# Where the quadrant sums of a split-precision trunk are computed: 128 additions of 128x512 elements between GpSimd and VectorE

## The chip, the core and the metric

One core of one Trainium2 chip runs the whole program. The metric is device time in microseconds (us) of one execution, as the median of several. An engine name in a row is one of PE (TensorE's matmuls), PEld (TensorE's weight loads), DVE (VectorE), ACT (ScalarE), POOL (GpSimd) and SP (SyncE, which here issues the DMAs).

## What is computed

One layer of a trunk on 1024 tokens of 1024 channels, all in fp32:

```python
h = rms_norm(x, norm_mix_pre)
y = hybrid_mixer(h, w_in, ...)          # four mixers on one input projection, gates, w_out
x = x + rms_norm(y, norm_mix_post)
h = rms_norm(x, norm_ffn_pre)
gt, up = split(h @ w_ffn_in, 2)
x = x + rms_norm((silu(gt) * up) @ w_ffn_out, norm_ffn_post)
```

The input projection has 6912 columns (`w_in`), the FFN 2816 hidden channels. Each `rms_norm` multiplies by a factor per channel at its end.

## The kernel before

**Precision.** Every fp32 operand of a matmul is split in two (`split`, L133 to L137): ACT casts it to a reduced type (`hi`, L135), DVE subtracts that from the source (`lo`, L136), and three matmuls (hi by hi, hi by lo, lo by hi; L210 to L212, in the last product L1226 to L1228) take the place of one. So each operand costs an ACT cast and then a DVE subtraction before PE can use it. The split of a weight goes into a ring of three buffers (`whi`, `wlo`), so it can be at most three units of weights ahead of PE.

**Strassen's form.** Most of the two large products (from `w_in` and `w_ffn_in`) and all of the last one (`w_ffn_out`) are computed in Winograd's form of Strassen's method: seven block products in place of eight, on sums and differences of quadrants. Those sums are elementwise work. Three places make them.

- `token_sums` (L277 to L304) makes the four sums T1 to T4 of the tokens' quadrants, in four steps. A step adds the hi and lo of four quadrants back together into `x11`, `x12`, `x22`, `x21` (L296, four instructions), combines them on DVE (L297 to L300), and splits the four results (L136, tiles `T1h`, `T1l` and so on). It runs twice: at the start of the input projection (about 22 to 78 us in the profile) and at the start of the FFN (868 to 950 us). It runs interleaved with plain projections, whose weights (`wlo_av` of `raw_av`, and `wlo_fu` of `raw_fu`) are split by the same two engines.
- `column_sums` (L307 to L320) makes the sums of the weights for `wino`; that stays on POOL (L318).
- `ffn_out` (L1165 on) computes the last product. It takes the 22 blocks of 128 hidden channels as 11 pairs, in three chunks of 4, 4 and 3 pairs. In a chunk, `pairs_` holds two tiles `af` of activations and two of weights (`wf`, or `raw_fo` for the first two) for each pair, and a pair's operands are 128x512 quadrants A11 to A22 and B11 to B22. Seven products m1 to m7 follow each other; each takes one unit per pair (`units`: the split of one A and one B quadrant into `whi_fo`, `wlo_fo`) and 12 matmuls per unit. After the first product `sums1` (L1192) makes four sums of the pair (L1196 to L1199), and after the second `sums2` (L1202) four more (L1205 to L1208); the other five products use those. A finished product is added to `ya`, the result, by DVE (L1260) or in the first chunk partly copied by ACT (L1258).

In the last chunk the end of the layer is interleaved: when a half (512 channels) of a token tile is complete, `half_done` (L1266) takes its sum of squares on ACT (L1270), multiplies it by the channel factors `gf` of the last norm (L1271: the first half of a tile on POOL, the second on DVE), computes the reciprocal root on POOL (L1274, L1280, L1282), scales and adds the residual on DVE (L1285), and SP stores it (L1286).

**Order.** A scheduler sorts the instructions of each engine when the program is built; each engine then goes through its own queue strictly in that order. Priorities steer it: `tc.high_priority(n)` lets code be placed as if it had been written n steps earlier (AHEAD_SPLIT = 160 for splits and for the sums of `ffn_out`, AHEAD_SUM = 400 for `column_sums`). So when an operation changes its engine, the order around it changes too.

Of the kernel before, what the change touches and what calls it, by code (L numbers as in the profile page):

```python
# [13 lines left out]
ALU = mybir.AluOpType  # L14
# [24 lines left out]
def hybrid_trunk(ctx, tc, x, w_in, w_branch, w_out, w_ffn_in, w_ffn_out, cols, gpost, gfpost,  # L39
                 abias, wst, bsr, wabd, wxbd, lvl, tril, eye, out, dbg=None):  # L40
    nc = tc.nc
# [38 lines left out]
    def slot(name, dt=F32, w=D):  # L80
        cnt[0] += 1
        t = sp.tile([P, D], dt, tag="S", name=f"{name}_{cnt[0]}", bufs=NSLOT)
        return t[:, :w]
# [17 lines left out]
    def small(name, w):  # L101
        cnt[0] += 1
        return sm.tile([P, w], F32, tag=f"s{w}", name=f"{name}_{cnt[0]}", bufs={1: 24, 8: 8}.get(w, 4))
# [29 lines left out]
    def split(src, hi, lo, scale=None):  # L133
        if scale is None:
            nc.scalar.copy(hi, src)  # L135
            return nc.vector.tensor_tensor(lo, src, hi.bitcast(F32), op=ALU.subtract)  # L136
        else:  # L137
            nc.scalar.activation(hi, src, AF.Copy, scale=scale)
            return nc.vector.scalar_tensor_tensor(lo, src, scale, hi.bitcast(F32), op0=ALU.mult, op1=ALU.subtract)
# [129 lines left out]
    halfs = [slice(0, 512), slice(512, 1024)]  # L269

    def wtmp(name, dt=F32):
        cnt[0] += 1
        return scope["p"].tile([P, 512], dt, tag="w", name=f"{name}_{cnt[0]}", bufs=8)

    def b_quad(zs, i, j):
        return [lambda kk, z=z: z(4 * (i - 1) + kk, halfs[j - 1]) for z in zs]

    def token_sums(ops, *zs):
        T = {}
        for n in ("B11", "B12", "B21", "B22"):  # L280
            ops[n] = b_quad(zs, int(n[1]), int(n[2]))
        for n in ("T1", "T2", "T3", "T4"):
            T[n] = {}
            ops[n] = [lambda kk, n=n, z=z: T[n][kk // 2][z][:, (kk % 2) * 512 : (kk % 2) * 512 + 512] for z in range(2)]
        for kk in range(4):
            if kk % 2 == 0:
                for n in T:
                    T[n][kk // 2] = (slot(f"{n}h", F32R), slot(f"{n}l", F32R))

            def q(name, z):  # L290
                return ops[name][z](kk).bitcast(F32)


            x11, x12, x22, x21 = (wtmp(f"x{n}") for n in ("11", "12", "22", "21"))
            for n, t in (("B11", x11), ("B12", x12), ("B22", x22), ("B21", x21)):
                nc.gpsimd.tensor_tensor(t, q(n, 0), q(n, 1), op=ALU.add)  # L296
            nc.vector.tensor_tensor(x12, x12, x11, op=ALU.subtract)  # L297
            nc.vector.tensor_tensor(x22, x22, x12, op=ALU.subtract)
            nc.vector.tensor_tensor(x11, x22, x11, op=ALU.subtract)
            nc.vector.tensor_tensor(x21, x22, x21, op=ALU.subtract)  # L300
            t1, t2, t3, t4 = x12, x22, x11, x21
            for n, t in zip(T, (t1, t2, t3, t4)):
                last[1] = split(t, ops[n][0](kk), ops[n][1](kk))
            yield  # L304
# [625 lines left out]
    interleave(first_norm(), proj_tm("bi", copy_to))  # L930
    started.append(1)
    interleave(seq(proj_tm("av", copy_to), proj_tm("cv", twice_gelu)), token_sums(ops1, hTh, hTl), 2, 1)

    away = {}
# [233 lines left out]
    def ffn_out(chunk, first, final):  # L1168
        n = len(chunk)
        pairs_ = []  # L1170
        for i, p in enumerate(chunk):
# [12 lines left out]
            q = {}  # L1184
            for nm, t in (("A", a), ("B", w)):
                for u in range(2):
                    for h in range(2):
                        r, c_ = (h, u) if nm == "A" else (u, h)
# [2 lines left out]

        def sums1(q):  # L1192
            q["S1"], q["T2"] = wtmp("s1"), wtmp("t2")
            gt_ = nc.gpsimd.tensor_tensor
            with tc.high_priority(AHEAD_SPLIT):
                gt_(q["S1"], q["A21"], q["A22"], op=ALU.add)  # L1196
                gt_(q["A11"], q["S1"], q["A11"], op=ALU.subtract)  # L1197
                gt_(q["B11"], q["B12"], q["B11"], op=ALU.subtract)
                gt_(q["T2"], q["B22"], q["B11"], op=ALU.subtract)  # L1199
            q["S2"], q["T1"] = q["A11"], q["B11"]  # L1200

        def sums2(q):  # L1202
            gt_ = nc.gpsimd.tensor_tensor
            with tc.high_priority(AHEAD_SPLIT):
                gt_(q["A21"], q["A22"], q["S2"], op=ALU.subtract)  # L1205
                gt_(q["B12"], q["B22"], q["B12"], op=ALU.subtract)
                gt_(q["A12"], q["A12"], q["S2"], op=ALU.subtract)  # L1207
                gt_(q["B21"], q["B21"], q["T2"], op=ALU.subtract)  # L1208
            q["S3"], q["T3"], q["S4"], q["T4n"] = q["A21"], q["B12"], q["A12"], q["B21"]
# [56 lines left out]
        def half_done(tt, c_, second):  # L1266

            y = yacc[tt][:, halfs[c_]]
            ss = small("yss", 1)
            nc.scalar.activation(junk[:, :512], y, AF.Square, accum_out=ss)  # L1270
            (nc.vector if second else nc.gpsimd).tensor_tensor(y, y, gf[:, halfs[c_]], op=ALU.mult)  # L1271
            if not second:
                early[tt] = small("ms0", 1)
                nc.gpsimd.tensor_scalar(early[tt], ss, 1.0 / D, EPS, op0=ALU.mult, op1=ALU.add)  # L1274
                xts_[tt] = slot("x1b")
                with tc.high_priority(AHEAD_OUT):
                    nc.sync.dma_start(xts_[tt], x1s[tt])
                return
            ms = small("ms", 1)
            nc.gpsimd.tensor_scalar(ms, ss, 1.0 / D, early[tt], op0=ALU.mult, op1=ALU.add)  # L1280
            r = small("rstd", 1)
            nc.gpsimd.tensor_tensor(r, ms, neghalf[:, :1], op=ALU.pow)  # L1282
            for cs in (halfs[1 - c_], halfs[c_]):
                xt = xts_[tt][:, cs]
                nc.vector.scalar_tensor_tensor(xt, yacc[tt][:, cs], r, xt, op0=ALU.mult, op1=ALU.add)  # L1285
                nc.sync.dma_start(out[tt * P : (tt + 1) * P, cs], xt)  # L1286
# [4 lines left out]
        def into_last(r, c_, second):  # L1291

            ev = into(r, c_, (r, c_) == (0, 1))

            def evl(t, ps):
                ev(t, ps)
                if final:
                    half_done(4 * r + t, c_, second)

            return evl  # L1300
# [4 lines left out]
        m4 = lambda: prod(ps2, "A22", "T4n", into_last(1, 0, True), more=True)  # L1305
        m3 = lambda: prod(ps1, "S4", "B22", into_last(0, 1, True), more=True)
        prod(ps1, "A11", "B11", into(0, 0, True), after=sums1)
        prod(ps2, "A12", "B21", into_last(0, 0, False), after=sums2)
        for m in ((m6, m5, m3, m7, m4) if final else (m6, m7, m5, m4, m3)):
            m()  # L1310

    pl = ffn_plain(0, *ffn_raw(0))
    interleave(take(pl, 4), second_norm(1), n_front=4)
    interleave(pl, token_sums(ops2, h2h, h2l))
    for g in range(1, NG):
        rg, ru = ffn_raw(g)
# [4 lines left out]
    gf = slot("gfpost")  # L1321
# [66 lines left out]
```

## Time and profile before

| | |
|---|---|
| three runs | 1584.7, 1588.14, 1587.63 us (median 1587.63) |
| the profiled execution | 1582.72 us, of which the span from first to last instruction is 1580.9 us |
| TensorE's mean granted clock | 0.987 of full speed |
| busy share of the span | PE 96%, PEld 80%, DVE 67%, ACT 36%, POOL 37% |

The busy shares are means over stages that differ. The rows further down come from these views: the waits of an engine (what it waited for, total us, times, longest); windows (for each stretch of time: its length, then busy us and, in brackets, instructions of PE, PEld, DVE, ACT and POOL, then the granted clock of TensorE, the DMA engines' share and GB/s); timelines (start, duration, engine, line, operation, output and input; the part in brackets is the idle time before and who ended it); and groups of instructions (line, engine, operation, tiles, shapes and count, then total busy us, mean ns of one, and idle time before). A DVE row's duration reaches past the start of the next one, so the price of one in a full queue is the pitch from start to start.

### The profile page before, as it was taken

The numbers are of one execution on the slowest core, as the hardware profiler recorded it, in microseconds if no ns is written. First come the engines' busy times: TensorE is split into PE (matmuls) and PEld (weight loads), VectorE is DVE, ScalarE is ACT, GpSimd is POOL, SyncE is SP. The second block draws the span as 40 slices with busy tenths as digits, with TensorE's granted clock in tenths as the row PEclk, the third lists the DMA queues.
The fourth block names the chain that finished last, engine by engine and source line by source line (L and its number), as shares of the span: only waits on it lengthen the run. The fifth ranks groups of instructions, "written<-read, shape, count | busy, mean of one in ns | idle before, by whom it ended". The sixth has DMA issues, their size and how long they took to land. (4 is left out here: it accounts for less than half of the span.)

```text
span 1580.9 us, 20619 instructions
## 1 busy us (share of the span) xinstructions
PE 1512.4 (96%) x7876; PEld 1258.2 (80%) x7876; DVE 1056.4 (67%) x1456; ACT 568.7 (36%) x942; POOL 589.7 (37%) x471
## 2 busy tenths in 40 slices
PE   7899999999999999999999989999999999898986
PEld 7898888888887878766899868888888887686865
DVE  5976674444469566988846694555555557779898
ACT  6433343333320352345335532222232223443533
POOL 2565333333100100332613364333333336639194
PEclk9899999999999999999999999999999999999998
DMA  6324333333461147563126312222222246420212
GB/s 233 108 91 154 124 114 107 113 107 107 151 218 65 68 153 259 190 250 132 56 80 240 114 40 80 80 82 85 80 83 93 91 134 241 148 104 27 81 54 107
DMA packets 108548, 191.49 MB, mean 121 GB/s; under 512 B 6432, under 2 KB 65440, under 8 KB 108448
## 3 DMA queue, kind: packets, MB, share of 16 engines
q1 hardware_dynamic: 108448, 190.16, 34.6%
q8 instruction: 62, 1.02, 0.3%
q14 instruction: 38, 0.31, 0.1%
HBM read 136.66 MB, written 53.48 MB: 120 GB/s over the span
## 5 line engine op out<-in xcount | busy, mean ns | idle before, releaser
L136 DVE TENSOR_TENSOR wlo_ws<-s,whi_ws 128x1024 fp32r<-128x1024 f32 x76 | 115.3, 1518 | 56.4 <-ACT whi_ws L135 56.4
L355 DVE TENSOR_TENSOR u<-u,mm_w 128x512 f32<-128x512 f32 x38 | 26.1, 686 | 173.7 <-PE mm_w L212 173.7
L135 ACT CAST whi_ws<-s 128x1024 fp32r<-128x1024 f32 x76 | 80.1, 1054 | 154.9 <-PE mm_w L211 137.9
L1227 PE MATMUL mm_fo<-wlo_fo,whi_fo 128*128 128x512 f32 x308 | 122.9, 401 | 12.6 <-DVE wlo_fo L136 12.6
L318 POOL TENSOR_TENSOR s<-raw_pj 128x512 f32<-128x512 f32 x38 | 59.9, 1577 | 197.3 <-DMA raw_pj<-in_w_in 184.7
L1228 PE MATMUL mm_fo<-whi_fo,wlo_fo 128*128 128x512 f32 x308 | 119.2, 396 | 0.0
L318 POOL TENSOR_TENSOR s<-raw_fu 128x512 f32<-128x512 f32 x19 | 32.9, 1731 | 198.2 <-DMA raw_fu<-in_w_ffn_in 198.2
L1226 PE MATMUL mm_fo<-whi_fo 128*128 128x512 f32 x308 | 93.5, 396 | 9.3 <-ACT whi_fo L135 8.0
L136 DVE TENSOR_TENSOR wlo_fo<-af,whi_fo 128x512 fp32r<-128x512 f32 x66 | 72.9, 1112 | 26.1 <-ACT whi_fo L135 25.7
L1227 PEld LDWEIGHTS mm_fo<-wlo_fo,whi_fo 128*128 128x128 f32 x308 | 58.7, 191 | 31.3 <-DVE wlo_fo L136 19.4
L135 ACT CAST whi_fo<-af 128x512 fp32r<-128x512 f32 x66 | 40.6, 622 | 107.6 <-PE mm_fo L1228 56.7
L339 ACT COPY m<-mm_w 128x512 f32<-128x512 f32 x38 | 22.3, 586 | 155.7 <-PE mm_w L212 142.2
L1226 PEld LDWEIGHTS mm_fo<-whi_fo 128*128 128x128 f32 x308 | 58.6, 190 | 23.6 <-ACT whi_fo L135 9.3
L211 PE MATMUL mm_wo<-wlo_wo,mh 128*128 128x256 f32 x256 | 72.3, 284 | 1.7 <-DVE wlo_wo L136 1.7
L212 PE MATMUL mm_wo<-whi_wo,ml 128*128 128x256 f32 x256 | 72.4, 284 | 1.2 <-DVE ml L917 1.2
L210 PE MATMUL mm_wo<-whi_wo,mh 128*128 128x256 f32 x256 | 71.5, 284 | 0.6 <-ACT whi_wo L135 0.6
L1228 PEld LDWEIGHTS mm_fo<-whi_fo,wlo_fo 128*128 128x128 f32 x308 | 59.1, 192 | 12.1
L210 PE MATMUL mm_w<-hTh,whi_wa 128*128 128x512 f32 x152 | 59.1, 389 | 0.0
L211 PE MATMUL mm_w<-hTl,whi_wa 128*128 128x512 f32 x152 | 59.1, 389 | 0.0
L210 PE MATMUL mm_w<-T3h,whi_ws 128*128 128x512 f32 x152 | 59.1, 389 | 0.0
L212 PE MATMUL mm_w<-T4h,a 128*128 128x512 f32 x152 | 59.1, 389 | 0.0
L212 PE MATMUL mm_w<-h2h,wlo_wa 128*128 128x512 f32 x152 | 59.1, 389 | 0.0
(386 smaller groups left out, 4769.7 us busy)
## 6 DMA issues: line engine op xcount, KB each, us to landing
raw_pj<-in_w_in SPq DMA_DIRECT2D x19, 1024.0 KB, 5.9
gt<-st_g SPq DMA_DIRECT2D x22, 512.0 KB, 5.2
raw_fg<-in_w_ffn_in SPq DMA_DIRECT2D x11, 1024.0 KB, 4.9
raw_fu<-in_w_ffn_in SPq DMA_DIRECT2D x11, 1024.0 KB, 5.5
af<-act SPq DMA_DIRECT2D x22, 512.0 KB, 4.1
wf<-in_w_ffn_out SPq DMA_DIRECT2D x18, 512.0 KB, 6.1
xt<-in_x SPq DMA_DIRECT2D x16, 512.0 KB, 8.0
raw_wo<-in_w_out SPq DMA_DIRECT2D x8, 1024.0 KB, 5.1
```

The costliest lines, as they stand in the source:

```text
L135: nc.scalar.copy(hi, src)
L136: return nc.vector.tensor_tensor(lo, src, hi.bitcast(F32), op=ALU.subtract)
L210: nc.tensor.matmul(ps, lhsT=lh(k), rhs=rh(k), start=(not more and k == 0), stop=False, skip_group_check=more)
L211: nc.tensor.matmul(ps, lhsT=lh(k), rhs=rl(k), start=False, stop=False, skip_group_check=more)
L212: nc.tensor.matmul(ps, lhsT=ll(k), rhs=rh(k), start=False, stop=(k == n - 1), skip_group_check=more)
L318: last_sum[0] = nc.gpsimd.tensor_tensor(out_, x0, x1_, op=op)
L339: nc.scalar.copy(m1, p1)
L355: nc.vector.tensor_tensor(u2, u2, p3, op=ALU.add)
L1226: nc.tensor.matmul(ps, lhsT=hi[:, ts], rhs=hi[:, 512:1024], start=start, stop=False, skip_group_check=more)
L1227: nc.tensor.matmul(ps, lhsT=hi[:, ts], rhs=lo[:, 512:1024], start=False, stop=False, skip_group_check=more)
L1228: nc.tensor.matmul(ps, lhsT=lo[:, ts], rhs=hi[:, 512:1024], start=False, stop=stop, skip_group_check=more)
```

## The change

The additions of L296 (16 per call of `token_sums`, two calls), the eight sums per pair in `ffn_out` (11 pairs) and the eight first-half multiplications of L1271 are issued on DVE in place of POOL: 32 + 88 + 8 = 128 instructions of 128x512 elements in fp32. Nothing else is edited.

```diff
--- before.py
+++ after.py
@@ -293,7 +293,7 @@
 
             x11, x12, x22, x21 = (wtmp(f"x{n}") for n in ("11", "12", "22", "21"))
             for n, t in (("B11", x11), ("B12", x12), ("B22", x22), ("B21", x21)):
-                nc.gpsimd.tensor_tensor(t, q(n, 0), q(n, 1), op=ALU.add)
+                nc.vector.tensor_tensor(t, q(n, 0), q(n, 1), op=ALU.add)
             nc.vector.tensor_tensor(x12, x12, x11, op=ALU.subtract)
             nc.vector.tensor_tensor(x22, x22, x12, op=ALU.subtract)
             nc.vector.tensor_tensor(x11, x22, x11, op=ALU.subtract)
@@ -1191,7 +1191,7 @@
 
         def sums1(q):
             q["S1"], q["T2"] = wtmp("s1"), wtmp("t2")
-            gt_ = nc.gpsimd.tensor_tensor
+            gt_ = nc.vector.tensor_tensor
             with tc.high_priority(AHEAD_SPLIT):
                 gt_(q["S1"], q["A21"], q["A22"], op=ALU.add)
                 gt_(q["A11"], q["S1"], q["A11"], op=ALU.subtract)
@@ -1200,7 +1200,7 @@
             q["S2"], q["T1"] = q["A11"], q["B11"]
 
         def sums2(q):
-            gt_ = nc.gpsimd.tensor_tensor
+            gt_ = nc.vector.tensor_tensor
             with tc.high_priority(AHEAD_SPLIT):
                 gt_(q["A21"], q["A22"], q["S2"], op=ALU.subtract)
                 gt_(q["B12"], q["B22"], q["B12"], op=ALU.subtract)
@@ -1268,7 +1268,7 @@
             y = yacc[tt][:, halfs[c_]]
             ss = small("yss", 1)
             nc.scalar.activation(junk[:, :512], y, AF.Square, accum_out=ss)
-            (nc.vector if second else nc.gpsimd).tensor_tensor(y, y, gf[:, halfs[c_]], op=ALU.mult)
+            nc.vector.tensor_tensor(y, y, gf[:, halfs[c_]], op=ALU.mult)
             if not second:
                 early[tt] = small("ms0", 1)
                 nc.gpsimd.tensor_scalar(early[tt], ss, 1.0 / D, EPS, op0=ALU.mult, op1=ALU.add)
```

The scheduler then sorts DVE's queue anew. Two places, with the rows of DVE's queue as the built program has them (line, operation, output<-inputs, shape).

The first is DVE in the first `token_sums`, from the end of the last norm tile to the split `wlo_av` of the second half of the weight `raw_av`. Before:

```order
L388 SCALAR_TENSOR_TENSOR hTl13_67_388<-mx_tr_81_487,ident_cv_89,hTh13_66_385 128x256 x2
L298 TENSOR_TENSOR x22_100_671<-x22_100_671,x12_99_670 128x512
L136 TENSOR_TENSOR T1l_91_662<-x12_99_670,T1h_90_661 128x512
L299 TENSOR_TENSOR x11_98_669<-x22_100_671,x11_98_669 128x512
L300 TENSOR_TENSOR x21_101_672<-x22_100_671,x21_101_672 128x512
L136 TENSOR_TENSOR T2l_93_664<-x22_100_671,T2h_92_663 128x512
L136 TENSOR_TENSOR T3l_95_666<-x11_98_669,T3h_94_665 128x512
L136 TENSOR_TENSOR T4l_97_668<-x21_101_672,T4h_96_667 128x512
L297 TENSOR_TENSOR x12_107_795<-x12_107_795,x11_106_794 128x512
L136 TENSOR_TENSOR wlo_av_85_553<-raw_av_9_100,whi_av_85_552 128x1024
```

After the change:

```order
L388 SCALAR_TENSOR_TENSOR hTl13_67_388<-mx_tr_81_487,ident_cv_89,hTh13_66_385 128x256 x2
L296 TENSOR_TENSOR x22_100_671<-hTh12_63_374,hTl12_64_377 128x512
L296 TENSOR_TENSOR x21_101_672<-hTh02_25_149,hTl02_26_152 128x512
L296 TENSOR_TENSOR x11_106_794<-hTh00_19_127,hTl00_20_130 128x512
L296 TENSOR_TENSOR x12_107_795<-hTh10_57_352,hTl10_58_355 128x512
L296 TENSOR_TENSOR x22_108_796<-hTh12_63_374,hTl12_64_377 128x512
L296 TENSOR_TENSOR x21_109_797<-hTh02_25_149,hTl02_26_152 128x512
L136 TENSOR_TENSOR T1l_91_662<-x12_99_670,T1h_90_661 128x512
L298 TENSOR_TENSOR x22_100_671<-x22_100_671,x12_99_670 128x512
L297 TENSOR_TENSOR x12_107_795<-x12_107_795,x11_106_794 128x512
L136 TENSOR_TENSOR wlo_av_85_553<-raw_av_9_100,whi_av_85_552 128x1024
```

Eight instructions stood between `hTl13` and `wlo_av`, among them all four splits of the first step; now nine stand there, six of them additions of L296, and the splits T2 to T4 come behind `wlo_av`.

The second is DVE in chunk 3 of `ffn_out`, around the unit 1863 (product m6, third pair), whose A operand is the tile `af_1819` after L1197. Before:

```order
L136 TENSOR_TENSOR wlo_fo_1869_12505<-s1_1836_12290,whi_fo_1868_12504 128x512
L136 TENSOR_TENSOR wlo_fo_1869_12505<-wf_1817_12246,whi_fo_1868_12504 128x512
L1260 TENSOR_TENSOR ya3_1690_11009<-ya3_1690_11009,mm_fo7_1830_12265 128x512
L136 TENSOR_TENSOR wlo_fo_1863_12453<-t2_1839_12297,whi_fo_1863_12452 128x512
L136 TENSOR_TENSOR wlo_fo_1872_12511<-s1_1838_12296,whi_fo_1871_12510 128x512
L136 TENSOR_TENSOR wlo_fo_1872_12511<-wf_1821_12254,whi_fo_1871_12510 128x512
L136 TENSOR_TENSOR wlo_fo_1890_12659<-af_1811_12234,whi_fo_1889_12658 128x512
L136 TENSOR_TENSOR wlo_fo_1890_12659<-wf_1813_12238,whi_fo_1889_12658 128x512
L136 TENSOR_TENSOR wlo_fo_1893_12665<-af_1815_12242,whi_fo_1892_12664 128x512
L136 TENSOR_TENSOR wlo_fo_1893_12665<-wf_1817_12246,whi_fo_1892_12664 128x512
L136 TENSOR_TENSOR wlo_fo_1863_12453<-af_1819_12250,whi_fo_1863_12452 128x512
```

After the change:

```order
L136 TENSOR_TENSOR wlo_fo_1869_12505<-s1_1836_12290,whi_fo_1868_12504 128x512
L136 TENSOR_TENSOR wlo_fo_1869_12505<-wf_1817_12246,whi_fo_1868_12504 128x512
L1260 TENSOR_TENSOR ya0_1687_11006<-ya0_1687_11006,mm_fo4_1827_12262 128x512
L136 TENSOR_TENSOR wlo_fo_1863_12453<-t2_1839_12297,whi_fo_1863_12452 128x512
L136 TENSOR_TENSOR wlo_fo_1872_12511<-s1_1838_12296,whi_fo_1871_12510 128x512
L1260 TENSOR_TENSOR ya1_1688_11007<-ya1_1688_11007,mm_fo5_1828_12263 128x512
L136 TENSOR_TENSOR wlo_fo_1872_12511<-wf_1821_12254,whi_fo_1871_12510 128x512
L1205 TENSOR_TENSOR af_1819_12250<-af_1820_12251,af_1819_12250 128x512
L1207 TENSOR_TENSOR af_1820_12251<-af_1820_12251,af_1819_12250 128x512
L136 TENSOR_TENSOR wlo_fo_1890_12659<-af_1811_12234,whi_fo_1889_12658 128x512
L1260 TENSOR_TENSOR ya2_1689_11008<-ya2_1689_11008,mm_fo6_1829_12264 128x512
L136 TENSOR_TENSOR wlo_fo_1863_12453<-af_1819_12250,whi_fo_1863_12452 128x512
```

The two sums L1205 and L1207 of the third pair, which were on POOL, stand in the same queue now, and two splits fewer and one addition L1260 more stand ahead of the last row. Further up in the queue, between the splits of the units ahead of this one, the other sums of the chunk stand in the same way.

## Rows read from the trace of the kernel before

**Rows 1.** The page: busy us (share of span) and instructions of TensorE.
```profile
PE 1512.4 (96%) x7876; PEld 1258.2 (80%) x7876; DVE 1056.4 (67%) x1456; ACT 568.7 (36%) x942; POOL 589.7 (37%) x471
```

**Rows 2.** Waits of PE, 0 to 85, 880 to 960, 1310 to 1581: total us, times, longest.
```profile
PE mm_av L211 <- DVE wlo_av L136: 6.6, 1, 6.6
...
PE mm_fu L212 <- DVE wlo_fu L136: 4.2, 2, 3.4
...
PE mm_fo L1227 <- DVE wlo_fo L136: 12.6, 15, 4.4
PE mm_fo L1226 <- ACT whi_fo L135: 8.0, 3, 3.9
```

**Rows 3.** Windows around the first token sums; the third is undisturbed.
```profile
40.00:60.00 20.00, 12.56 (x95) 12.15 (x94) 20.00 (x18) 6.71 (x11) 17.48 (x11) 0.82 0.25 87
60.00:80.00 20.00, 20.00 (x157) 20.00 (x156) 19.97 (x35) 10.54 (x19) 5.72 (x4) 0.92 0.35 122
80.00:100.00 20.00, 20.00 (x169) 20.00 (x168) 14.58 (x48) 6.22 (x11) 6.77 (x8) 1.00 0.32 106
```

**Rows 4.** Windows around the second token sums; the first is undisturbed.
```profile
920.00:924.00 4.00, 4.00 (x19) 3.16 (x17) 3.90 (x3) 0.60 (x2) 4.00 (x3) 1.00 0.00 0
924.00:928.00 4.00, 0.63 (x2) 0.42 (x2) 3.97 (x5) 3.22 (x6) 0.51 (x1) 0.84 0.01 2
928.00:932.00 4.00, 4.00 (x10) 3.05 (x10) 4.00 (x5) 0.00 (x0) 3.16 (x3) 0.50 0.78 246
932.00:936.00 4.00, 4.00 (x16) 3.25 (x15) 4.00 (x5) 1.89 (x3) 2.23 (x2) 0.81 0.22 82
```

**Rows 5.** Windows in the last product; the second is undisturbed.
```profile
1350.00:1360.00 10.00, 7.71 (x32) 5.39 (x30) 10.00 (x11) 1.76 (x3) 10.00 (x7) 1.00 0.25 102
1370.00:1380.00 10.00, 10.00 (x46) 8.26 (x45) 6.60 (x10) 5.42 (x11) 0.44 (x1) 1.00 0.51 168
```

**Rows 6.** Timeline of PE: before and at the last product's start, chunk 3's start, the end.
```profile
1318.78 0.39 PE L210 MATMUL mm_w<-T3h,whi_ws 128*128 128x512 f32 x1
...
1323.09 0.39 PE L1226 MATMUL mm_fo<-whi_fo 128*128 128x512 f32 x1
...
1499.61 0.84 PE L1226 MATMUL mm_fo<-whi_fo 128*128 128x512 f32 x3
...
1567.53 0.39 PE L1228 MATMUL mm_fo<-whi_fo,wlo_fo 128*128 128x512 f32 x1
```

**Rows 7.** Timeline of DVE, first token sums: start, duration, work, [idle before, releaser].
```profile
41.91 0.86 DVE L388 SCALAR_TENSOR_TENSOR hTl<-mx_tr,ident_cv,hTh 128x256 fp32r<-128x256 f32 x2
...
48.73 1.77 DVE L136 TENSOR_TENSOR T2l<-x,T2h 128x512 fp32r<-128x512 f32 x1
...
55.45 2.28 DVE L136 TENSOR_TENSOR wlo_av<-raw_av,whi_av 128x1024 fp32r<-128x1024 f32 x1
...
58.25 0.68 DVE L136 TENSOR_TENSOR T1l<-x,T1h 128x512 fp32r<-128x512 f32 x1
58.85 0.68 DVE L299 TENSOR_TENSOR x<-x,x 128x512 f32<-128x512 f32 x1
```

**Rows 8.** Timeline of DVE, second token sums.
```profile
909.72 0.87 DVE L388 SCALAR_TENSOR_TENSOR h2l<-mx_tr,ident_cv,h2h 128x256 fp32r<-128x256 f32 x2
...
926.31 1.22 DVE L136 TENSOR_TENSOR wlo_fu<-raw_fu,whi_fu 128x1024 fp32r<-128x1024 f32 x1
```

**Rows 9.** Groups by line and form, 1310 to 1581.
```profile
L1260 DVE TENSOR_TENSOR ya<-ya,mm_fo 128x512 f32<-128x512 f32 x68 | 43.1, 676 | 1.8 <-PE mm_fo L1228 1.8
```

**Rows 10.** Operation by line: L1196 on POOL, ns min/median/max.
```profile
L1196 POOL TENSOR_TENSOR s<-af,af x11: 1291/1739/1838, 1323.4 to 1514.5; 128x512 f32<-128x512 f32 x11
```

**Rows 11.** Timeline of ACT and DVE around 1364: a sum's cast and its split.
```profile
1364.13 1.14 ACT L135 CAST whi_fo<-af 128x512 fp32r<-128x512 f32 x2 [5.68 <-POOL af L1197]
...
1364.78 2.81 DVE L136 TENSOR_TENSOR wlo_fo<-af,whi_fo 128x512 fp32r<-128x512 f32 x2 [3.03 <-ACT whi_fo L135]
```

**Rows 12.** Timeline of DVE in the tail.
```profile
1570.05 1.43 DVE L1285 SCALAR_TENSOR_TENSOR x1b<-ya,rstd,x1b 128x512 f32<-128x512 f32 x2 [2.07 <-POOL rstd L1282]
```

## Prediction

> **What bounds the kernel now.** TensorE is busy 1512.4 us of the span of 1580.9 [rows 1], so a gain can only come from the 68 us in which it is not, or from stretches in which it runs below its clock. I looked first at what PE waits for. The large entries all name DVE's lo splits and ACT's casts, in three places: 6.6 us in one wait for `wlo_av`, 4.2 us for `wlo_fu`, and 12.6 and 8.0 us in the last product [rows 2]. These are the three places in which POOL makes sums.
>
> Windows then size each place. An undisturbed 20 us holds 169 matmuls of this stage; 40 to 60 has 95, 60 to 80 has 157, so 86 are missing, and 86 x 20/169 = **10.2 us** are lost [rows 3]. Part of it is the granted clock, whose means there are 0.82 and 0.92: after the wait PE works some us at the lower of its two levels. At the second token sums an undisturbed 4 us holds 19; 2, 10 and 16 follow, 29 are missing, 29 x 4/19 = **6.1 us**, with the clock at 0.50, the 1.2 GHz level, in 928 to 932, after PE had been busy for 0.63 of 4 us [rows 4]. In the last product I count by the pitch of a matmul: 19 start between 1318.78 and 1323.09, so 0.2268 us each [rows 6]. From 1323.09 to 1499.61 PE runs 684 matmuls (672 of two chunks, 12 left over from before): 176.5 - 155.1 = **21.4 us** lost. From there to 1567.76, one pitch after the last start, it runs 252: 68.2 - 57.2 = **11.0 us** [rows 6]. That makes 48.7 us over the three places. The tail, from there to the end of the span, is 13.1 us.
>
> Why are the splits late? Where POOL adds, a DVE instruction of 128x512 with two operands in SBUF takes 1.77 us, and one of 128x1024 2.28; a moment later, with POOL idle, 0.68 (0.60 from start to start) and 1.22 [rows 7, 8]. POOL's own addition takes 1.29 at the least and 1.74 in the median [rows 10]. So the two engines take turns. Additions into `ya`, with one operand in PSUM, have 676 ns in the mean, POOL or not [rows 9]. DVE's 10.00 busy in 1350 to 1360 is eleven instructions [rows 5]: it is full of waiting, not of work.
>
> **The change, part by part.** 128 POOL instructions leave. Each lengthened a DVE instruction beside it by 1.70 - 0.60 = 1.1 us; in its place DVE gets one more at 0.60. That price is not shown for these lines on DVE, but L299 and the T splits have the same form (two fp32 operands in SBUF, 128x512), and theirs is the nearest row: 0.60 [rows 7], which I take. The upper bound is 1.70, what such an instruction costs now. Where nothing else hides it, an instruction that reads the result of the one just before it must wait for its end too, 0.68 and a little more.
>
> *First token sums (16 additions).* After the change nine instructions stand between the last norm tile's `hTl13` and `wlo_av`. The L388 pair ends at 42.8 [rows 7]; one addition has come ahead of it, 0.6; nine at 0.60 are 5.4, then 1.22: `wlo_av` ends at 50.0. Now it ends at 55.45 + 2.28 = 57.7, and PE wanted it 6.6 earlier, at 51.1 [rows 2, 7]. The wait goes, and with it the low clock behind it. The later splits of this stage were pushed back by the same sums and move forward too. What stays is the cast on ACT, under 1 us. Gain 9.5 of 10.2. Up to 0.72 us for each of the nine, `wlo_av` would still be on time.
>
> *Second token sums (16).* The last L388 pair ends at 910.6 [rows 8]; the changed queue has thirteen instructions of 0.60 after it; one addition has come ahead of it (0.6) and a lengthened L297 there is short again (1.1): 910.1 + 7.8 + 1.2 = 919.1. Now `wlo_fu` ends at 927.5, and PE wanted it at 924.1 [rows 2, 8]. Gain 5.5 of 6.1; POOL's column sums (L318) remain and still lengthen a few splits here.
>
> *The last product (88 sums).* DVE's stock of work by chunk at 0.60, with 0.61 for an addition into `ya`: chunk 1 has 56 splits, 12 additions, 32 sums, 60 us; chunk 2 has 56, 28 and 32, 70 us; chunk 3 has 42, 28, 24, the 16 of L1271 and 16 of L1285 (0.68), 77 us. PE's work is 76.2 (336 matmuls) in each of the first two and 57.2 in the third, which has the tail of 13 behind it. So DVE has room in chunks 1 and 2 and is about as long as PE with its tail in chunk 3. Within chunk 2 the sums crowd the first half: between the splits of the units 1787 and 1792 DVE's queue has 29 instructions, 17.5 us, for five units of 12 matmuls, 13.6 us, and the ring allows a lead of at most three units; I leave a wait of 3 us there, and 4 for the turns between chunks, where PE must wait for additions queued behind sums. Gain 21.4 - 7 = 14. In chunk 3, from the split of its first unit, 1831, to that of unit 1863, DVE has 30 us of instructions; PE has these units and the three between to do, five in all, 13.6, and DVE's lead by the ring is worth two to three units, 5.4 to 8.2. So PE waits there about 8 to 11 us, much as now. Gain 11.0 - 9 = 2.
>
> *The eight of L1271.* In the tail DVE gets four instructions more, 2.4 us. Against that stand its idle 2.07 us, waiting for the reciprocal root that POOL made late behind L1271 [rows 12]. I take zero, between +2.4 and -2.1.
>
> *Nothing else* has a price: POOL's column sums, norms and gates keep their places, and between the first two and the last of these places (about 100 to 870 and 960 to 1310 us) the four engines' queues are in the same order as before.
>
> Sum: 9.5 + 5.5 + 14 + 2 = **31 us**. From the profiled execution's 1582.72 (its span of 1580.9 and 1.8 around it, which nothing here touches) that gives 1551.7; the median of the runs is 4.9 above that execution, so I forecast 1587.63 - 31 = **1556.6 us**. Bounds by the trace: the 48.7 us back and 2.1 in the tail, 1537; nothing back at all and 0.60 for each of the 120 sums, 1660.
>
> In 1350 to 1360 DVE is busy all of the time [rows 5]. The Trainium skill, in "Perfetto Trace Analysis", section "Optimizing Scalar/DVE Operations", says that where DVE is saturated it may make sense to hand work to another engine, even GpSimd; the change does the reverse in just such stretches, and by that sentence alone the sum would be the 1660 above. The same place adds that the two share a port, so that moving work between them might not help. Rows 7 take the second side: the busy share is made of instructions of 1.77 that are 0.60 without POOL.
>
> **Rivals.** *DVE becomes the bound (slower).* Place: the last product, where DVE must do 342 instructions in stretches that now last 176.5 us (chunks 1 and 2) and 81.3 (chunk 3 with its tail), 258 together. A sum, its cast on ACT and its split follow each other across engines: 0.65 us from cast to split [rows 11], and DVE's queue stands still meanwhile unless something else is queued. If such turns lift the mean price of a DVE instruction from 0.61 to 0.85, the product takes 342 x 0.85 = 291, 33 more than now, less the 15 of the token sums: 1587.6 + 18 = 1606. It decides at (258 + 15)/342 = 0.80. Against it: in the order shown, other splits stand between a sum and its reader. This is what the skill's sentence would make of the kernel. Chance 0.05.
>
> *Only the token sums gain.* The queue in the last product loses as much by sums in front of splits as it wins: 1587.6 - 15 = 1572.6. For it: 4.8 us of sums per pair, in order, ahead of splits; chunk 3's count. Against it: 10 and 6 us of room in chunks 1 and 2. Chance 0.12.
>
> *Nearly all comes back.* If the sums fall into DVE's idle moments and chunk 3 is fed early: 1587.6 - 46 = 1541.6. For it: DVE was idle 3.4 of 10 us where POOL was quiet [rows 5]. Against it: chunk 3's 30 us of queue. Chance 0.12.
>
> *The change does nothing*, because a later transfer or PE's own order takes the place of each wait: within 0.2% (3.2 us, about what a measurement of this kernel can tell from no change). Chance 0.03; the loads of the last product have landed before they are wanted, since no wait of PE's, DVE's or ACT's of any size names one.
>
> **How the numbers follow.** The forecast's case, a gain of 20 to 43 us, has 0.68. Faster by over 0.2%: 0.68 + 0.12 + 0.12 = 0.92; same 0.03; slower 0.05. The range goes from 1545, some way to the case of nearly all, up to 1574, which takes in the case of the token sums alone; outside lie half of the former, the slow case, and no change.
>
> **What would show it.** Right: `wlo_av` and `wlo_fu` of 1.22 us and no wait of PE for them; no lower clock in those windows; DVE's splits in the last product near 0.68 us each; waits of PE left mainly at chunk 2's start and in chunk 3; a tail of 12 to 14 us. Wrong: splits over 1 us with POOL quiet (then the turns were not POOL's), idle time of DVE before ACT's casts that grows by tens of us (the slow rival), or PE losing over 25 us in the last product.

## The result, and the profile after

Before 1587.3 us, after **1547.88 us** (medians of four runs each): the ratio is 0.9755, with a 95% interval of 0.9738 to 0.9772. That is 39 us less. The profiled execution of the kernel after took 1548.8 us with a span of 1547.0. Measured again beside other kernels (e9, below) the ratio was 0.9769 [0.9755, 0.9782]. The two profiled executions are 34 us apart. Single executions of one kernel lie up to 5 us apart (the kernel before, fifteen times beside e1 to e4: 1582.44 to 1587.19), so the stages below are counted in the profiles.

The page of the kernel after, the same row as [rows 1]:

```profile
PE 1502.6 (97%) x7876; PEld 1255.8 (81%) x7876; DVE 1037.1 (67%) x1584; ACT 567.5 (37%) x942; POOL 393.5 (25%) x343
```

PE's waits in the three places, in the order of [rows 2]. The columns are total us, times, and the longest:

```profile
PE mx_tr L378 <- DVE xn L368: 7.7, 2, 7.4
PE mm_bi L212 <- DVE hTl L388: 0.8, 3, 0.4
...
PE mx_tr L378 <- DVE xn L368: 2.6, 1, 2.6
...
PE mm_fo L1227 <- DVE wlo_fo L136: 3.8, 2, 2.5
PE mm_fo L1226 <- DVE ya L1260: 3.2, 2, 2.0
PE mm_fo L1226 <- ACT whi_fo L135: 1.3, 4, 0.3
```

The waits for `wlo_av` and `wlo_fu` are gone (what is left of those two stretches, but for waits of under 1 us, is the norm's `xn`, which was there before), and the last product's 20.6 us of waits for splits and casts have become 8.3, of which 3.2 are now for additions into `ya`.

DVE's own rows show why. Its timeline at the two token sums, as in [rows 7] and [rows 8]:

```profile
43.76 3.70 DVE L296 TENSOR_TENSOR x<-hTh,hTl 128x512 f32<-128x512 f32 x6
...
49.48 1.23 DVE L136 TENSOR_TENSOR wlo_av<-raw_av,whi_av 128x1024 fp32r<-128x1024 f32 x1 [0.21 <-ACT whi_av L135]
...
913.45 1.22 DVE L136 TENSOR_TENSOR wlo_fu<-raw_fu,whi_fu 128x1024 fp32r<-128x1024 f32 x1
```

Six additions of L296 take 3.70 us together, 0.60 from start to start, and both weight splits take 1.23 and 1.22. `wlo_av` ends at 50.7 in place of 57.7. In the last product the groups by line and form, as in [rows 9], with the mean ns after the comma; the first row is from before the change, the others from after it:

```profile
L136 DVE TENSOR_TENSOR wlo_fo<-af,whi_fo 128x512 fp32r<-128x512 f32 x66 | 72.9, 1112 | 26.1 <-ACT whi_fo L135 25.7
```
```profile
L136 DVE TENSOR_TENSOR wlo_fo<-af,whi_fo 128x512 fp32r<-128x512 f32 x66 | 45.9, 696 | 17.6 <-ACT whi_fo L135 17.4
L1260 DVE TENSOR_TENSOR ya<-ya,mm_fo 128x512 f32<-128x512 f32 x68 | 44.2, 689 | 1.6 <-PE mm_fo L1228 1.4
...
L1271 DVE TENSOR_TENSOR ya<-ya,gfpost 128x512 f32<-128x512 f32 x16 | 10.8, 694 | 0.8 <-ACT junk L1270 0.8
...
L1196 DVE TENSOR_TENSOR s<-af,af 128x512 f32<-128x512 f32 x11 | 7.6, 688 | 0.0
```

The splits of `af` had a mean of 1112 ns before and have 696 now; the moved lines last the same 0.69 us. The windows, first around the first token sums ([rows 3]), then the second ([rows 4]):

```profile
40.00:60.00 20.00, 20.00 (x169) 20.00 (x168) 19.79 (x34) 9.24 (x18) 0.00 (x0) 1.00 0.52 186
60.00:80.00 20.00, 20.00 (x169) 20.00 (x169) 18.04 (x37) 9.76 (x17) 1.17 (x3) 1.00 0.34 112
...
912.00:916.00 4.00, 4.00 (x20) 3.30 (x18) 4.00 (x7) 4.00 (x8) 0.00 (x0) 1.00 0.06 10
916.00:920.00 4.00, 4.00 (x19) 3.34 (x18) 4.00 (x7) 1.81 (x4) 0.00 (x0) 1.00 0.95 304
```

PE has its full 169 in each 20 us and 19 to 20 in each 4, at the full clock. The last product's first and last matmul, as in [rows 6]:

```profile
1309.49 0.39 PE L1226 MATMUL mm_fo<-whi_fo 128*128 128x512 f32 x1
...
1534.03 0.39 PE L1228 MATMUL mm_fo<-whi_fo,wlo_fo 128*128 128x512 f32 x1
```

With one pitch after the last start that is 224.8 us against 244.7. Where the 34 us of the profiles came from, by the first start of each product's matmuls:

| stretch, from the first matmul of one product to that of the next | before | after | gained |
|---|---|---|---|
| start to the first Strassen product | 100.1 | 91.2 | 8.9 |
| from there to the gates' products | 359.1 | 363.3 | **-4.3** |
| gates to the product of `w_out` | 323.9 | 323.5 | 0.4 |
| `w_out` to the FFN's first Strassen product | 181.0 | 172.5 | 8.5 |
| from there to the last product | 359.0 | 359.0 | 0.0 |
| last product | 244.7 | 224.8 | 19.9 |
| tail | 13.1 | 12.7 | 0.4 |

Half of what the first token sums won is given back at once. These windows and timelines of PE and of DVE, of the kernel after, show where:

```profile
92.00:96.00 4.00, 4.00 (x20) 3.29 (x19) 3.90 (x6) 1.65 (x3) 3.92 (x4) 1.00 0.00 0
96.00:100.00 4.00, 1.49 (x6) 0.99 (x5) 3.93 (x8) 1.30 (x2) 2.10 (x2) 0.91 0.81 243
100.00:104.00 4.00, 4.00 (x13) 3.11 (x13) 4.00 (x6) 1.11 (x2) 2.32 (x2) 0.67 0.25 87
```
```profile
96.62 0.39 PE L212 MATMUL mm_w<-T4h,a 128*128 128x512 f32 x1
99.52 0.80 PE L212 MATMUL mm_w<-T2h,wlo_ws 128*128 128x512 f32 x1 [2.51 <-DVE wlo_ws L136]
...
96.94 1.20 DVE L1005 TENSOR_SCALAR svs<-svs 128x2 f32<-128x2 f32 x1
...
98.25 1.22 DVE L136 TENSOR_TENSOR wlo_ws<-s,whi_ws 128x1024 fp32r<-128x1024 f32 x1
```

PE waits 2.51 us for `wlo_ws`, the split of the first column sums, and then works at a lower granted clock for a while (mean 0.67 in 100 to 104, between its two levels of 1.2 and 2.4 GHz). The sums themselves were not late. These rows of POOL and ACT, of the kernel after, show it, and the last, of DVE in the kernel before, is the same split:

```profile
82.73 1.30 POOL L318 TENSOR_TENSOR s<-s,raw_pj 128x512 f32<-128x512 f32 x1
89.17 1.53 POOL L318 TENSOR_TENSOR s<-raw_pj 128x512 f32<-128x512 f32 x1 [5.14 <-ACT tg L413]
...
96.85 1.25 POOL L318 TENSOR_TENSOR s<-raw_pj,s 128x512 f32<-128x512 f32 x1
```
```profile
91.89 1.04 ACT L135 CAST whi_ws<-s 128x1024 fp32r<-128x1024 f32 x1
```
```profile
99.96 1.70 DVE L136 TENSOR_TENSOR wlo_ws<-s,whi_ws 128x1024 fp32r<-128x1024 f32 x1 [1.79 <-ACT whi_ws L135]
```

The two sums of this split end at 84.0 and its cast at 92.9, but the split starts only at 98.25. Until then it stands in DVE's queue behind a chain of very small instructions (`svs`, 128x2 elements), and the next six column sums on POOL, from 89.2 to 98.1, make six of its last eight links last 1.15 to 1.26 us in place of 0.16. In the kernel before, POOL was quiet from 85.6 to 98.0, the chain was over at 91.8, and the split waited for its cast alone. So it is contention once more, at a place where it had cost nothing.

### The profile page after: what moved, and what is told of

Same layout as the page of the kernel before. It is cut to its first block, busy times and chain, and to the rows that moved or that the text cites. A ratio compares the mean times of both kernels' runs of the same rounds, so it can differ in the third digit from the quotient of the medians.

```text
span 1547.0 us, 20559 instructions
## 1 busy us (share of the span) xinstructions
PE 1502.6 (97%) x7876; PEld 1255.8 (81%) x7876; DVE 1037.1 (67%) x1584; ACT 567.5 (37%) x942; POOL 393.5 (25%) x343
## 4 chain that ended last, share of the span: by engine, by line
PE 84%; DVE 11%; issue 2%; ACT 1%; POOL 1%; DMA 1%; DVEq 0%; SPq 0%; ACTq 0%; POOLq 0%
PE mm_w L212 16%; PE mm_w L211 16%; PE mm_w L210 15%; PE mm_fo L1227 3%; PE mm_fo L1228 3%; PE mm_fo L1226 3%; PE mm_gate L210 2%; PE mm_gate L212 2%; PE mm_gate L211 2%; PE mm_proj L210 2%; PE mm_proj L211 1%; PE mm_proj L212 1%; PE mm_wo L211 1%; PE mm_wo L212 1%; PE mm_wo L210 1%
## 5 line engine op out<-in xcount | busy, mean ns | idle before, releaser
L136 DVE TENSOR_TENSOR wlo_ws<-s,whi_ws 128x1024 fp32r<-128x1024 f32 x76 | 109.9, 1446 | 53.0 <-ACT whi_ws L135 53.0
L318 POOL TENSOR_TENSOR s<-raw_fu 128x512 f32<-128x512 f32 x19 | 39.6, 2085 | 223.6 <-DMA raw_fu<-in_w_ffn_in 223.6
L1226 PEld LDWEIGHTS mm_fo<-whi_fo 128*128 128x128 f32 x308 | 57.7, 188 | 18.8 <-ACT whi_fo L135 3.0
L1274 POOL TENSOR_SCALAR ms<-yss 128x1 f32<-128x1 f32 x8 | 9.3, 1157 | 227.8 <-ACT junk L1270 227.7
L212 PE MATMUL mm_w<-T2h,wlo_ws 128*128 128x512 f32 x152 | 60.0, 395 | 2.5 <-DVE wlo_ws L136 2.5
L211 PE MATMUL mm_w<-T2l,whi_ws 128*128 128x512 f32 x152 | 59.6, 392 | 0.0
L210 PE MATMUL mm_w<-T2h,whi_ws 128*128 128x512 f32 x152 | 59.6, 392 | 0.0
```

What stands on the lines that cost most here:

```text
L210: nc.tensor.matmul(ps, lhsT=lh(k), rhs=rh(k), start=(not more and k == 0), stop=False, skip_group_check=more)
L211: nc.tensor.matmul(ps, lhsT=lh(k), rhs=rl(k), start=False, stop=False, skip_group_check=more)
L212: nc.tensor.matmul(ps, lhsT=ll(k), rhs=rh(k), start=False, stop=(k == n - 1), skip_group_check=more)
L318: last_sum[0] = nc.gpsimd.tensor_tensor(out_, x0, x1_, op=op)
L1226: nc.tensor.matmul(ps, lhsT=hi[:, ts], rhs=hi[:, 512:1024], start=start, stop=False, skip_group_check=more)
```

## The experiments

My theory: GpSimd's additions lengthen VectorE's instructions (contention), and that is what PE waited for. Rivals: the sums themselves came late from a full GpSimd; VectorE is near to being the bound; the parts work on each other. In each experiment, time is told as the median beside that of the kernel before on the same chip, and stages from the profile. e4 to e7 are one execution each.

**e1: token sums alone.**

```diff
-                nc.gpsimd.tensor_tensor(t, q(n, 0), q(n, 1), op=ALU.add)
+                nc.vector.tensor_tensor(t, q(n, 0), q(n, 1), op=ALU.add)
```

> Only the 32 additions of L296 on VectorE; the sums of the last product and L1271 stay on GpSimd. If the parts add up, this gives what the profile after shows ahead of the last product: 13.6 us (the last product's first matmul moved from 1323.1 to 1309.5), so about 1574 against 1587. The last product keeps its 244.7 us and its tail of 13.1. If instead the order of the last product depended on the earlier stages, its length would move by several us.

Measured: 1568.6 against 1585.47, ratio 0.9894 [0.9879, 0.9909], 17 us. In its profile the last product's first matmul starts at 1309.9, 13.2 us earlier than in the first profile of the kernel before and 15.0 earlier than in the second (e4); about 1574 was expected. The last product takes 244.7 us and the tail 13.1, as before. So the token sums do not work on the later stages.

**e2: the last product's sums alone.** In `sums1` and `sums2`:

```diff
-            gt_ = nc.gpsimd.tensor_tensor
+            gt_ = nc.vector.tensor_tensor
```

> Only the 88 sums of the last product on VectorE. If the parts add up: the last product takes 224.8 us in place of 244.7, so 20 us, about 1567; PE's waits for wlo_av (6.6) and wlo_fu (4.2) stay, and so do splits of 1.77 us at the token sums. If GpSimd's first-half multiplications in the tail matter beside the sums, the tail is over 14 us.

Measured: 1566.51 against 1585.47, ratio 0.9882 [0.9868, 0.9895], 19 us. The last product takes 225.9 us, its first matmul starts at 1324.8, and the tail is 13.2.

**e3: the channel factors alone.**

```diff
-            (nc.vector if second else nc.gpsimd).tensor_tensor(y, y, gf[:, halfs[c_]], op=ALU.mult)
+            nc.vector.tensor_tensor(y, y, gf[:, halfs[c_]], op=ALU.mult)
```

> Only the eight first halves of L1271 on VectorE. My term was zero, between 2.4 us longer and 2.1 shorter; the tail of the profile after is 0.4 us shorter than before. Expected: 1587, within 2 us. If the contention with these eight was worth something in chunk 3, up to 8 x 1.1 = 9 us shorter.

Measured: 1586.37 against 1585.47, ratio 1.0005 [0.9996, 1.0014]. Nothing. Together the three parts give 17 + 19 - 1 = 35 us, against 34 in the profiles and 37 to 39 in the medians of the whole.

**e4: the kernel before once more.** No edit.

> The kernel before, unchanged, with a second profile. The medians are 39 us apart, the two profiled executions 34; the profiled execution of before was 4.6 us under its median. If a stage varies from run to run, this profile shows where: the last product longer than 244.7 us, or the losses at the token sums over 10.2 and 6.1. If the spread is outside the span, the stages repeat within 1 us.

Measured: one execution of 1584.69 with a span of 1582.9. Its last product takes 244.8 us, the tail 13.2, and the first Strassen product starts at 100.1, all within 0.4 us of the first profile. The stretch from the gates to `w_out` is 0.9 shorter, and the one from `w_out` to the FFN 2.6 longer: there PE's two waits for `wlo_fu` take 7.0 us in place of 4.2. So the stages repeat within 1 us, but for the second token sums, where the wait itself varies.

**e5: no sums.** `sums1` and `sums2` are reduced to names, here the first:

```diff
-                gt_(q["S1"], q["A21"], q["A22"], op=ALU.add)
...
-            q["S2"], q["T1"] = q["A11"], q["B11"]
+            q["S1"], q["T2"], q["S2"], q["T1"] = q["A21"], q["B22"], q["A11"], q["B11"]
```

> The kernel before with the eight sums per pair of the last product left out: its seven products use quadrants of the inputs as they are, so the result differs. Token sums and L1271 stay on GpSimd. Every split and matmul of the last product stays. Both theories expect the same: PE nearly full, the last product 213 to 222 us in place of 244.6, splits near 0.69 us.

Measured: 1550.58 against 1585.07. The last product takes 212.2 us, just under the range expected, which is 936 matmuls at 0.2268 (212.3; its own 924 and 12 left over) and nothing else. So all 32 us that the kernel before lost there come with the sums.

**e6: sums that nobody reads.** As e5, and in `sums1` (in `sums2` in the same way):

```diff
+            q["x"], q["y"] = wtmp("s1"), wtmp("t2")
...
+                gt_(q["x"], q["A21"], q["A22"], op=ALU.add)
+                gt_(q["x"], q["x"], q["A11"], op=ALU.subtract)
+                gt_(q["y"], q["B12"], q["B11"], op=ALU.subtract)
+                gt_(q["y"], q["B22"], q["y"], op=ALU.subtract)
...
```

> As e5 (the products use the inputs' quadrants as they are), but GpSimd still does the 88 additions of 128x512, into tiles that nothing else reads. Theory of contention: each of them holds back a split on VectorE by 1.1 us although nobody waits for its result, so the last product comes back to 236 to 246 us, with splits over 1 us in the mean. Rival, lateness: before the change the sums themselves came late, because GpSimd was full with them and took 1.74 us for each; then, with no reader, the last product stays within 4 us of e5.

Measured: 1583.58 against 1585.07. The last product takes 245.5 us, as before, though no cast, split or matmul reads a sum. The groups by line and form of e6, then its waits of PE, then a window:

```profile
L136 DVE TENSOR_TENSOR wlo_fo<-af,whi_fo 128x512 fp32r<-128x512 f32 x77 | 90.9, 1180 | 13.2 <-ACT whi_fo L135 13.1
...
L1260 DVE TENSOR_TENSOR ya<-ya,mm_fo 128x512 f32<-128x512 f32 x68 | 43.2, 676 | 3.1 <-PE mm_fo L1228 3.0
...
L1205 POOL TENSOR_TENSOR s<-af,s 128x512 f32<-128x512 f32 x11 | 19.1, 1741 | 0.0
```
```profile
PE mm_fo L1227 <- DVE wlo_fo L136: 20.7, 36, 2.0
```
```profile
1350.00:1360.00 10.00, 9.05 (x36) 6.53 (x36) 10.00 (x11) 3.22 (x7) 10.00 (x7) 1.00 0.47 191
```

And the same split in e5:

```profile
L136 DVE TENSOR_TENSOR wlo_fo<-af,whi_fo 128x512 fp32r<-128x512 f32 x77 | 54.5, 708 | 57.0 <-ACT whi_fo L135 56.6
```

The splits have 1180 ns in the mean with GpSimd at work and 708 without; the additions into `ya`, which read PSUM, have 676 with and 679 without. In ten us VectorE does eleven instructions, GpSimd seven. So contention alone is enough for a loss of this size. It is not shown that all of the loss before the change was of this kind: there 8.0 of the 20.6 us of PE's waits were for casts [rows 2], and casts did wait for sums on GpSimd [rows 11]. In e6 such waits are gone and those for splits are longer, 20.7 in place of 12.6. What share late sums had in the kernel before stays open.

**e7: each sum twice on VectorE.** From the kernel after, in `sums1` (likewise in `sums2`):

```diff
+                gt_(q["T2"], q["A21"], q["A22"], op=ALU.add)
                 gt_(q["S1"], q["A21"], q["A22"], op=ALU.add)
+                gt_(q["T2"], q["S1"], q["A11"], op=ALU.subtract)
                 gt_(q["A11"], q["S1"], q["A11"], op=ALU.subtract)
...
```

> The kernel after with each of the 88 sums of the last product computed twice on VectorE, the first time into a place that is overwritten. It tests the rival by which VectorE becomes the bound: 430 instructions of 0.605 us are 260 us, as long as the stretch before the change (244.6 and the tail of 13.2). If VectorE sets the pace at that point, the last product takes 224.7 + 20 to 35. If it has room for them beside PE, it stays under 235; by my count by chunk there are 3, -13 and -22 us of room, so I expect the former.

Measured: 1576.31 against 1585.07. The last product takes 255.8 us, 31 more than in the kernel after and 11 more than before the change. PE's waits in e7, and one of its windows (the columns as above: length, then PE, PEld, DVE, ACT, POOL):

```profile
PE mm_fo L1233 <- DVE wlo_fo L136: 13.1, 9, 3.0
PE mm_fo L1232 <- ACT whi_fo L135: 7.8, 7, 5.7
PE mm_fo L1232 <- DVE ya L1266: 7.0, 6, 2.9
```
```profile
1400.00:1450.00 50.00, 44.64 (x183) 34.57 (x183) 49.61 (x83) 18.57 (x33) 0.00 (x0) 0.97 0.14 50
```
```profile
1400.00:1450.00 50.00, 48.05 (x202) 38.67 (x202) 45.44 (x76) 21.52 (x38) 0.00 (x0) 0.97 0.12 42
```

The second window is that of the kernel after. Over the whole last product VectorE is busy 252.5 of 255.7 us in e7 and 197.3 of 224.5 in the kernel after. So 88 more additions make it the bound: the slow rival is real, and the change stops short of it by less than the work it moved.

**e8 and e10: the first column sums on VectorE too.** From the kernel after, in `column_sums`:

```diff
-                    last_sum[0] = nc.gpsimd.tensor_tensor(out_, x0, x1_, op=op)
+                    last_sum[0] = (nc.gpsimd if n_cs[0] >= 2 else nc.vector).tensor_tensor(out_, x0, x1_, op=op)
+        n_cs[0] += 1
```

> The kernel after with the column sums (L318) of the first two calls of wino on VectorE too. After the change the first call of wino starts 8.9 us earlier but 4.5 us of that are lost again at 96 to 104 us, where PE waits 2.5 us for a split of the weights' sums and then runs at the lower clock. If the cause is GpSimd's sums, which come late there and hold VectorE's instructions back, 3 to 5 us come back: 1543 to 1545 against 1548. Rival: VectorE's queue is full there with other work; then within 1 us of the kernel after, or slower.

> The kernel after, unchanged, so that the three below are compared with it on one chip. Ratio to before 0.975 as before, spans by stage within 2 us of the profile after.

> The kernel of e8 again, beside the kernel after. Its first profile had the 4.3 us at 96 to 104 us back and nothing else changed; so 3 to 5 us under e9. If the difference of the spans was scatter, within 1 us of e9.

Measured: e8 1546.25 against 1585.07 for before, where 1543 to 1545 was expected, and its ratio of 0.9756 [0.9739, 0.9772] is that of the change itself; e9, the kernel after, 1548.4 and e10 1545.87 against 1585.46. In the profile of e8 the first Strassen product starts at 91.2, as in the kernel after, and the gates' products at 450.2 in place of 454.5: the 4.3 us are back. Its split of the column sums and its window:

```profile
91.59 1.22 DVE L136 TENSOR_TENSOR wlo_ws<-s,whi_ws 128x1024 fp32r<-128x1024 f32 x1
```
```profile
96.00:100.00 4.00, 4.00 (x19) 3.34 (x18) 3.90 (x7) 0.63 (x1) 3.80 (x3) 1.00 0.01 4
```

PE has no gap there now, and the split starts 6.7 us earlier than in the kernel after. In whole executions it is 2.5 us between e9 and e10, less than the 3 to 5 expected. The intervals of the ratios to before (0.9769 [0.9755, 0.9782] and 0.9751 [0.9737, 0.9764]) overlap, but all four executions of e10, up to 1546.37, lie under all four of e9, from 1546.92 on. The stage itself shows it: from the first Strassen product to the gates' products it is 359.1 us in e8 and e10, as before the change, and 362.0 in e9.

**e11: all column sums on VectorE.** The same line, always `nc.vector`.

> The kernel after with the column sums (L318) of all 38 calls of wino on VectorE, 152 additions of 128x512. By contention each holds back a VectorE instruction by up to 1.1 us, but PE waits for none of them beyond 110 us, and VectorE is busy for 5 to 6 tenths there. So the theory that only places where PE waits can gain expects the same as e10, within 2 us. If every GpSimd addition cost something, 152 x 0.1 or more: 15 us under e10.

Measured: 1545.68, as e10. Against the kernel after, 152 more additions have left GpSimd (its busy time fell from 393.5 us to 142.7), and the group of splits that had stood beside them became shorter, in the kernel after and in e11:

```profile
L136 DVE TENSOR_TENSOR wlo_ws<-s,whi_ws 128x1024 fp32r<-128x1024 f32 x76 | 109.9, 1446 | 53.0 <-ACT whi_ws L135 53.0
```
```profile
L136 DVE TENSOR_TENSOR wlo_ws<-s,whi_ws 128x1024 fp32r<-128x1024 f32 x76 | 92.9, 1223 | 39.2 <-ACT whi_ws L135 39.1
```

17 us less of busy time, and no time gained over e10, which had moved the first eight of the 152: PE waited for none of the rest.

**e12: sums placed earlier.** From e10, in `sums1` and `sums2`:

```diff
-            with tc.high_priority(AHEAD_SPLIT):
+            with tc.high_priority(250):
```

> The kernel of e10 with the sums of the last product at a priority of 250 in place of 160, so that some stand earlier in VectorE's queue. The last product still loses 12.4 us, by splits and additions behind sums. If the order of the sums decides that, the last product moves by 2 us or more from 224.8; if VectorE's amount of work decides, it stays within 1.

Measured: 1545.66, the last product 224.9 us, the waits as in the kernel after. But the edit moved little: of 335 instructions of VectorE in the last product, seven stand elsewhere than in e10, by one to three places. So whether the order of the sums decides the 12 us that are still lost there is not tested. e10 to e12 are the best versions here, at 0.975 of before, ahead of the kernel after by 2.5 us or so.

## Why the prediction was right, and where its sizes were off

The forecast was a gain of 31 us, 1556.6, in a range of 1545 to 1574; 1547.88 lies in it. The mechanism (GpSimd and VectorE taking turns, PE waiting for the lengthened splits) is what e5 and e6 show, as enough for a loss of this size. That the sum of 31 came within 3 us of the profiles' 34 is in part luck: 4.3 us were lost at a place that had no price, and the second token sums and the last product gave 3.0 and 3.9 more than forecast. Term by term, by the profiles:

- *The price of 0.60 for a moved addition* held: 3.70 us for six, and 688 to 699 ns long in the last product. `wlo_av` was forecast to end at 50.0 and ended at 50.7.
- *First token sums, 9.5.* The gain to the first Strassen product was 8.9, but the next line, that nothing else has a price, failed: with PE ahead, GpSimd's next column sums came to run beside a chain of small VectorE instructions, the split behind that chain came late, and 4.3 us went back. What contends next was asked of the splits of this stage and not of the product behind it. e8 and e10 show it by removing those sums from GpSimd.
- *Second token sums, 5.5.* The stretch gained 8.5. I had counted the matmuls missing in 924 to 936 only. The windows of the kernel before that I had passed over:

```profile
916.00:920.00 4.00, 2.84 (x13) 2.02 (x12) 4.00 (x4) 1.57 (x2) 4.00 (x4) 1.00 0.00 0
...
944.00:948.00 4.00, 3.19 (x15) 2.30 (x13) 4.00 (x7) 1.71 (x3) 0.00 (x0) 1.00 0.17 66
948.00:952.00 4.00, 3.95 (x17) 3.30 (x18) 3.53 (x5) 0.96 (x2) 0.00 (x0) 1.00 0.19 70
```

  With 19 as the full count, 6, 4 and 2 are missing there too, 12 x 4/19 = 2.5 us. PE waited there for a cast (`whi_fu`, 1.2 us) and for a split (`wlo_fu`, 0.9), and both waits went. With the scatter of 2.6 us that e4 shows in this stretch, the size is known to no better than that.
- *The last product, 14 + 2.* It gained 19.9. Chunks 1 and 2 kept about 6 of the 21.4 us lost, where I had left 7. Chunk 3 kept 6.5 where I had left 9, from a wait of 8 to 11 us at the unit 1863. Its incomplete windows, against a full count of 46, have 12, 12 and 6 missing, 30 x 10/46 = 6.5:

```profile
1490.00:1500.00 10.00, 7.87 (x34) 5.97 (x33) 10.00 (x18) 6.93 (x16) 2.25 (x4) 1.00 0.01 2
1500.00:1510.00 10.00, 7.53 (x34) 5.89 (x33) 10.00 (x17) 2.30 (x5) 3.64 (x1) 1.00 0.54 186
1520.00:1530.00 10.00, 8.83 (x40) 7.00 (x39) 9.88 (x16) 4.85 (x14) 5.90 (x10) 1.00 0.37 141
```

  The longest wait for a split in them is 2.47 us, in the place of that unit:

```profile
1503.64 0.50 PE L1227 MATMUL mm_fo<-wlo_fo,whi_fo 128*128 128x512 f32 x1 [2.47 <-DVE wlo_fo L136]
```

  The step that failed is "five units in all, 13.6": in PE's queue the three units of product m2 stand between as well, whose splits, in buffers of their own, had been made in chunk 2. So the limit of three units ahead, told above of the ring, does not hold for the products of chunk 3 that have buffers of their own (`spare`). In the built program 90 matmuls lie between the first of unit 1831 and the first of 1863, 20.4 us. With them the forecast's own sum, 30 less 20.4 and the lead of 5.4 to 8.2, would have given a wait of 1 to 4 us.
- *The tail, 0.* 0.4, and nothing that can be measured in e3.
- *The slow rival* put the point of decision at a mean price of 0.80 us for 342 instructions, 273 us of work. e7 shows that VectorE sets the pace at 430 x 0.605 = 260. The sentence of the Trainium skill, in "Perfetto Trace Analysis", section "Optimizing Scalar/DVE Operations", on handing work to GpSimd when VectorE is saturated, does not decide here: in e6 what looked saturated was in part waiting. The sentence next to it, that the two share a port and that moving work between them might not help, is the one with which the trace agrees (splits of 1180 ns beside GpSimd's additions, 708 without).
- The remaining gap, 39 us by the medians and 34 by the profiles, is not assigned to a stage. The profiled execution of the kernel before (1582.72) was faster than all four of its runs, that of the kernel after (1548.8) slower than two of its other three, and beside e9 the medians are 37 us apart.

## What to carry to other kernels

A VectorE busy for ten of ten us can be waiting for a third of them (eleven instructions of 0.60 us): look at the duration of one instruction with GpSimd at work and with GpSimd quiet, before calling it full and before giving GpSimd work to relieve it. Moving GpSimd's additions to VectorE pays only where something waits for VectorE beside them: 120 sums moved in three stretches gave 34 us, eight multiplications in the last chunk none, and 144 column sums none either. And when a stage moves forward, ask of the first thing behind it what will now run beside it.

## What was not expected of the hardware

Very small VectorE instructions are held back as much as large ones. In the timeline of the kernel after, beside GpSimd's column sums, an operation on 128x2 elements takes 1.23 us, and between two of them 0.16:

```profile
92.54 1.23 DVE L1005 TENSOR_SCALAR svs<-svs 128x2 f32<-128x2 f32 x1
93.80 0.16 DVE L1004 TENSOR_TENSOR svs<-svs 128x2 f32<-128x2 f32 x1
```

They are links of the chain of such instructions (L1004, L1005) that the first `wlo_ws` waited behind, so one that meets a GpSimd addition costs more than seven times its length. GpSimd's small instructions can be long too: the 128x1 scaling L1274 has 1157 ns in the mean after the change and had 538 before. But half of that mean is one instruction of 4.57 us, and the cause was not tested:

```profile
L1274 POOL TENSOR_SCALAR ms<-yss 128x1 f32<-128x1 f32 x8 | 9.3, 1157 | 227.8 <-ACT junk L1270 227.7
```
```profile
1499.07 4.57 POOL L1274 TENSOR_SCALAR ms<-yss 128x1 f32<-128x1 f32 x1 [1.23 <-ACT junk L1270]
```
